# A one-core hybrid decoder step: convolution's transfers on GpSimd's queue, two kpad tiles, parameters handed out by backlog, output matrices beside input matrices

## The chip, the cores and the metric

One NeuronCore of a Trainium2 chip runs the program; the metric is its device time in microseconds (us) per execution. The kernel before took 1393.75 us, the median of 3 runs (1392.28 to 1394.62). Engines are named as in the profile: PE is TensorE (PEld its weight loads), DVE is VectorE, ACT is ScalarE, POOL is GpSimd, SP is SyncE, which here only issues transfers (SPq).

## The reference

One inference step of a hybrid layer on 256 prompt positions and 64 sampled ones (8 sequences of 8), 320 columns in all, model width 2048, all in float32:

```python
h = rmsnorm(x, g_mix)
a_val, a_gate, b_u, b_v, c_u = jnp.split(h @ w_in, [512, 1024, 1536, 2048], axis=-1)
out_a = conformer_conv(a_val, a_gate, ...)    # GLU, causal depthwise conv of 31 taps, layernorm per head, silu
out_b = chunk_spatial_gate(b_u, b_v, ...)     # u * (lower-triangular W_s v + b) in chunks of 128
out_c = s5_branch(c_u, ...)                   # complex diagonal state space, 64 groups of 16 channels, 64 states each, GLU
x = x + concat(out_a, out_b, out_c) @ w_out
gate, up = jnp.split(rmsnorm(x, g_ffn) @ w_gu, 2, axis=-1)
x = x + (silu(gate) * up) @ w_down
y = rmsnorm(x, g_final)
```

It also returns the last 30 positions of the convolution's input, the states of the state-space branch and the normalized v of the sampled part.

## The kernel before, in words

**Units.** The projections are written as a list of units. A unit loads 512 KB of weights (8 blocks of 128x128 in float32), splits them into a high part on ScalarE (`split_hi`, line 203) and a low part on VectorE (`split_lo`, line 210), and multiplies three times: high by high, high by low, low by high (lines 237, 238, 240). Loads are issued by SP three units ahead (line 1291), the high split is made two units ahead, the low one unit ahead. A tile of 128 outputs takes two units. The planner counts a block of a unit as 0.44 us of TensorE (line 247).

**Order.** First come the projections of heads 0 and 1 of the convolution, interleaved, then the string `ORDER` (line 26): `C0..C7` are the tiles of the state-space branch, `A2`, `A3` the convolution heads 2 and 3 (four units each), `K0..K3` the convolutions as matrix products, `U0..U3` the gates of the spatial mixer, `V` its eight units for v. Then the output projection (from the state-space rows first, then from the rest), then gate and up, then down.

**The planner.** All else (norm, parameters, recurrence, layout changes) is written as Python generators, handed to a planner (`Side`, line 101). Four times per unit `side.run()` lets each task of priority below 1 that is due take one step, and tasks of priority 1 or more only while the planned time of VectorE, `V.t`, isn't ahead of that of TensorE, `side.pe`. `yield Wait(n)` puts a task off by n such steps. `Vec` (line 38) adds to `V.t` a cost for each instruction. All engines get their instructions in the order in which the planner wrote them; each runs its own in order, and so does each queue.

**Convolution.** When the value projection of head h is done, VectorE writes the tile `row`; `conv_in` (line 533) copies it to DRAM (`zr<-row`) and to the output (`out_rows<-row`), reloads `row` for head h+2, and reads it back as four copies `z<-zr` of 296 KB, one per 32 channels, each with 4 shifted views (access pattern `[[1, 4], [ZW, 32], [1, Z4]]`, line 547). All are issued by SP. There is one z4 tile, so the copies for head h wait for convolution h-1 to be written.

**State-space branch.** `params()` (line 452) hands out some 110 small instructions on VectorE, three per step: exponentials, sines, the powers of the decay, and last the factor k. With k, `bb_task` (line 642) makes the input matrices' base. `c_inputs` (line 714) makes input matrices for eight channel tiles, `c_states` (line 726) multiplies the inputs by them, `recurrence` (line 770) runs the scan on VectorE in two halves. `c_mats` (line 819) makes the output matrices: its task `pool` starts after the last input matrix (flag `P`), clears three tiles on GpSimd (line 833), and per tile makes products with the powers (`powers`, line 661), which ScalarE places. TensorE multiplies (line 867), and `mat_t` (line 873) writes the result into the tile `kpad` (ScalarE line 877, VectorE line 879), copies it to DRAM (`dk<-kpad`, line 887), and reads it back shifted (line 891). There is one `kpad` tile of 224 columns, 96 of them zeros. `c_out` (line 896) applies the matrices, `c_glu` (line 930) the gates, whose weights `c_glu_w` loads.

**Norm.** `norm_task` (line 476) squares x on ScalarE, adds the squares in tiles of 1280 columns on VectorE, and gives the factor that the gates and values of the first heads wait for.

Of the kernel before, what the change touches and what calls it, by code (L numbers as in the profile page):

```python
# [24 lines left out]

ORDER = "C0 C1 C2 K0 C3 C4 C5 C6 K1 C7 A2 U0 U1 K2 A3 V K3 U2 U3".split()

# [10 lines left out]
class Vec:  # L38
# [5 lines left out]
    def _add(self, out, fixed, per):  # L44
        n = 1
        for d in out.shape[1:]:
            n *= d
        self.t += fixed + per * n

# [105 lines left out]
def _build(ctx, nc, tc, I, O):  # L155
# [142 lines left out]
    G.memset(bbd, 0.0)  # L298
    kpad = tmp("kpad", (128, 7 * 32))
    G.memset(kpad[:, 0:96], 0.0)  # L300
    cent = kp.tile([128, 128], F32, name="cent")
# [96 lines left out]
    u1, u2 = pt(), pt()  # L398

    def cmul(o, x, y):  # L400
        E.tensor_tensor(u1, pw[:, 0, x, :], pw[:, 0, y, :], op=MULT)
        E.tensor_tensor(u2, pw[:, 1, x, :], pw[:, 1, y, :], op=MULT)
        E.tensor_tensor(pw[:, 0, o, :], u1, u2, op=SUB)
        E.tensor_tensor(u1, pw[:, 0, x, :], pw[:, 1, y, :], op=MULT)
        E.tensor_tensor(u2, pw[:, 1, x, :], pw[:, 0, y, :], op=MULT)
        E.tensor_tensor(pw[:, 1, o, :], u1, u2, op=ADD)

    cmul(2, 1, 1)
    cmul(3, 2, 1)
    cmul(4, 2, 2)  # L410

    apw = tmp("apw", (128, 3, 32, 8))
    apu = tmp("t1", (128, 256)).rearrange("p (i a b) -> p i a b", i=2, a=32)
    for i in range(2):
        E.tensor_copy(apw[:, 2 - i, :, 0], pw[:, i, 4, :])
    for n in (1, 2, 4):
        x = [apw[:, 2 - i, :, 0:n] for i in range(2)]
        y = [apw[:, 2 - i, :, n - 1:n].to_broadcast([128, 32, n]) for i in range(2)]
        v1, v2 = apu[:, 0, :, 0:n], apu[:, 1, :, 0:n]
        for i, j, op in ((0, 0, SUB), (1, 1, ADD)):  # L420
            E.tensor_tensor(v1, x[0], y[j], op=MULT)
            E.tensor_tensor(v2, x[1], y[1 - j], op=MULT)
            E.tensor_tensor(apw[:, 2 - i, :, n:2 * n], v1, v2, op=op)
    E.tensor_scalar(apw[:, 0], apw[:, 1], -1.0, None, op0=MULT)
    pr, kk = pt(), tmp("kk", (128, 2, 32))
    rd = tmp("rd", (128, 32))

# [11 lines left out]
    def k_params():  # L439
# [10 lines left out]
        E.tensor_tensor(kk[:, 1, :], u1, rd, op=MULT)  # L450

    def params():
        for i, f in enumerate(E.ops[8:]):
            f()
            if i % 3 == 2:
                yield Wait(1)
        S["kk"] = True

    rd_params(E)
    k_params()  # L460

# [66 lines left out]
    def row_load(h):  # L528

        S["row", h] = tmp("row", (128, ZW), bufs=2)  # L530
        nc.sync.dma_start(S["row", h], I["rows"][h])

    def conv_in(h):

        row = zrows[h]
        yield Wait(2)
        nc.sync.dma_start(row, S["row", h])
        nc.sync.dma_start(O["rows"][h], S["row", h])
        yield Wait(5)
        if h < 2:  # L540
            row_load(h + 2)
        while h and ("k", h - 1) not in S:
            yield Wait(1)
        z4 = S["z4", h] = tmp("z4", (128, 4, Z4))
        base = row[0:1, 0:1]
        for g in range(4):
            nc.sync.dma_start(z4[:, g], bass.AP(tensor=base.tensor, offset=base.offset + 32 * g * ZW,
                                                ap=[[1, 4], [ZW, 32], [1, Z4]]))

# [81 lines left out]
    def u_layout(ct, us, du):  # L631
        U = S["U"]
        yield Wait(2)
        nc.sync.dma_start(du[:, ct % 2], us)
        if ct % 2 == 1:
            yield Wait(5)
            for j in range(4):
                nc.sync.dma_start(U[32 * j:32 * j + 32, ct - 1:ct + 1],
                                  du[:, :, j, :].rearrange("(p g) t q -> g t p q", p=4))
            S["U due", ct // 2] = side.now + 4  # L640

    def bb_task():
        while "kk" not in S:
            yield Wait(1)
        bb = S["bb"] = tmp("bb", (128, 2, 32, 16))
        w12 = tmp("wv", (128, 2, 32, 16))
        w1, w2 = w12[:, 0], w12[:, 1]
        kr, ki = bc(kk[:, 0, :]), bc(kk[:, 1, :])
        for o, x, y, op in ((0, 0, 1, SUB), (1, 1, 0, ADD)):
            V.tensor_tensor(w1, kr, bld[:, x], op=MULT)  # L650
            yield None
            V.tensor_tensor(w2, ki, bld[:, y], op=MULT)
            yield "gap"
            V.tensor_tensor(bb[:, o], w1, w2, op=op)
            yield None
        h0 = S["h0"] = tmp("wv", (128, 1536))[:, 0:512].rearrange("p (a b c) -> p a b c", a=2, b=32)
        nc.gpsimd.dma_start(h0, I["h0"])
        side.add(0.6, c_states())
        side.add(0.7, c_mats())

    def powers(E, bd, ct, src, p0, step, tags):
# [13 lines left out]
        for o, x, y, op in ((0, 0, 1, SUB), (1, 1, 0, ADD)):  # L675
            t_ = tags[2 * o:2 * o + 2] if len(tags) == 4 else tags
            v1, v2 = (tmp(t, (128, 320 if t[0] == "g" else 256))[:, 0:64 * n].rearrange("p (a b c) -> p a b c", a=4, b=n) for t in t_)
            E.tensor_tensor(v1, pb(0), xb(x), op=MULT)
            yield None
            E.tensor_tensor(v2, pb(1), xb(y), op=MULT)  # L680
# [26 lines left out]
    def c_glu_w(ct):  # L707
        for k in (ct, ct + 1):
            if k < 8 and ("wg", k) not in S:
                S["wg", k] = tmp("wg", (128, 2, 128), bufs=2)  # L710
                nc.sync.dma_start(S["wg", k], I["wglu"][k])
        return S["wg", ct]

    def c_inputs():

        src = S["src"] = [S["bb"][:, :, 4 * ct:4 * ct + 4, :] for ct in range(8)]
        for ct in range(8):
            while ct - S["T"] >= 2:
                yield Wait(1)
            for y in powers(V, bds[ct % 2], ct, src[ct], 3, -1, ("t1", "t2", "g1", "g2")):  # L720
                if y == "place":
                    yield Wait(2)
            S["b due", ct] = side.now + 3
        S["P"] = True

    def c_states():
# [6 lines left out]
        for i in range(9):  # L733
            while i < 8 and side.now < S.get(("b due", i), 1e9):
                yield Wait(1)
            if i < 8:
                power0(bds[i % 2], S["src"][i], 3)
                yield Wait(2)
            ct = i - 1
            if ct >= 0:  # L740
# [78 lines left out]
    def c_mats():  # L819
# [8 lines left out]
        def pool():  # L828
            while "P" not in S:
                yield Wait(1)  # L830
            c_raw(0)
            for t in m[:3]:
                G.memset(t, 0.0)
                yield Wait(1)
            for ct in range(8):
                while S["pow0"] < ct:
                    yield Wait(1)
                raw[ct] = r = c_raw(ct)
                while ct >= 3 and "E" not in S or ct >= 5 and S["y"] < ct - 4:
# [8 lines left out]
                V.tensor_scalar(r[:, 1], r[:, 1], -1.0, None, op0=MULT)  # L848
                for y in powers(V, bd[ct], ct, r, 1, 1, ("t1", "t2", "g1", "g2") if ct < 5 else ("t1", "t2")):
                    if y == "place":  # L850
                        yield Wait(3)
                S["pow due", ct] = side.now + 1

        side.add(0.69, pool())
        for ct in range(8):
# [3 lines left out]
            while side.now < S.get(("pow due", ct), 1e9):  # L859
                yield Wait(1)  # L860
            power0(bd[ct], raw[ct], 0)
            S["pow0"] = ct + 1
            yield Wait(3)
            pr_ = sc()
# [8 lines left out]
    def mat_t(ct, pr_, bd, two):  # L873

        while ct and ("kpad", ct - 1) not in S:
            yield Wait(1)
        A.activation(kpad[:, 128:224], pr_[:, 32:128], AF.Copy)
        yield Wait(3)
        V.scalar_tensor_tensor(kpad[:, 96:128], id32, dsk[:, ct:ct + 1], pr_[:, 0:32], op0=MULT, op1=ADD)
        if ct in (0, 1, 5, 6):  # L880
            o = 512 * (ct % 5)
            Tt = two[:, o:o + 512].rearrange("p (a b) -> p a b", a=4)
        else:
            Tt = tmp("Tt", (128, 4, 128)) if ct in (2, 7) else tmp("P", (128, 4, 128), bufs=2)
        dk = dp.tile([128, 224], F32, tag="dk", name="dk")
        yield Wait(5)
        nc.sync.dma_start(dk, kpad)
        S["kpad", ct] = True
        yield Wait(1)
        for j in range(4):  # L890
            nc.sync.dma_start(Tt[32 * j:32 * j + 32],
                              dk[:, (3 - j) * 32:(3 - j) * 32 + 128].rearrange("(p g) x -> g p x", p=4))
        S["mats"][ct] = bd, Tt
# [78 lines left out]
    def b_load():  # L972
        t = tmp("z4", (128, 2, 4, 192))
        bs, wst = S["bs"], S["wst"] = t[:, 0], t[:, 1]
        nc.sync.dma_start(bs, I["bs"].partition_broadcast(128))
        nc.sync.dma_start(wst, I["wst"])
        side.add(0.8, b_mask())
# [110 lines left out]
    def need_x():  # L1088
        if "xa" not in X:
            X["xa"] = [a4(F32, "xa") for _ in range(4)]  # L1090
            X["row"] = [X["xa"][k // 4][:, k % 4, :] for k in range(KC)]
            for q in range(4):
                nc.gpsimd.dma_start(X["xa"][q], I["xT"][:, 4 * q:4 * q + 4, :])
            side.add(6, split_ab())
# [195 lines left out]
    for u, d in enumerate(units):  # L1290
# [25 lines left out]
        if u == 4:  # L1316
            A.activation(hbgl, bgl, AF.Copy, scale=0.5)
            A.activation(nhg, cv[:, :, 1:2], AF.Copy, scale=-0.5)
            A.activation(hb, cv[:, :, 2:3], AF.Copy, scale=0.5)
        if u == 2:  # L1320
            side.add(0.9, norm_task())
        if u == 2:
            nc.sync.dma_start(bld, I["s5b"])
            row_load(0)
            row_load(1)
        if u == 0:
            side.add(0.5, params())
        if u == 9:
            side.add(0.65, bb_task())
# [118 lines left out]
```

## Time and profile before

| | |
|---|---|
| median of 3 runs | 1393.75 us (1392.28 to 1394.62) |
| the profiled execution's own time | 1393.87 us |
| its span, first to last instruction | 1392.2 us |
| PE busy | 1328.8 us (95%), 9324 matmuls |
| DVE busy | 724.3 us (52%) |
| ACT busy | 564.0 us (41%) |
| POOL busy | 58.5 us (4%) |
| mean granted clock of PE | 0.976 of full speed |
| DMA | 212.76 MB, mean 153 GB/s |

A busy PE is not PE at its peak, as its matmuls are pipelined. The granted clock of a stretch is a share of 2.4 GHz; it has two levels, 1.0 and 0.5 (1.2 GHz), and a value between is a mean over a stretch with both. A wait is named by the engine, the tile it was about to write, the line, and what it waited for. The DMA share is the mean over 16 engines.

### The profile page before, as it was taken

To read this page: it belongs to the slowest core of one execution; us is meant where nothing else is said; L and a number is where in the kernel's file an instruction comes from. 1 tells how busy PE (TensorE), PEld (TensorE's weight loads), DVE (VectorE), ACT (ScalarE), POOL (GpSimd) and SP (SyncE) were. 2 spreads that over 40 slices of the span, in tenths; PEclk is the share of its full clock that TensorE was granted. 3 is DMA by queue.
4 is the path that set the end of the run, shared out by engine and by line. 5 is a ranking of instruction groups with operands and counts; after the bars stand their busy time and mean duration, and the time that the engine had idled before them with its cause. 6 is when DMAs were issued, how large, how long until landed. Compare 5 with 4: busy or idle time off the path is not lost.

```text
span 1392.2 us, 22691 instructions
## 1 busy us (share of the span) xinstructions
PE 1328.8 (95%) x9324; PEld 1297.0 (93%) x9324; DVE 724.3 (52%) x1201; ACT 564.0 (41%) x822; POOL 58.5 (4%) x75
## 2 busy tenths in 40 slices
PE   7869879699999999999999999999999999999995
PEld 7869868489999999999999999999999999999995
DVE  7946948547556444444444444444444444444444
ACT  6356535457345433333333333333333333333442
POOL 1010000002013000000000000000000000000112
PEclk9889989899999999999999999999999999999998
DMA  6455435556444444444444444455544444554553
GB/s 232 154 173 161 128 112 166 156 148 225 152 152 151 147 141 157 146 152 152 151 152 148 152 147 152 144 153 151 151 141 163 137 161 142 153 151 144 148 147 122
DMA packets 77912, 212.76 MB, mean 153 GB/s; under 512 B 17088, under 2 KB 25536, under 8 KB 77808
## 3 DMA queue, kind: packets, MB, share of 16 engines
q1 hardware_dynamic: 76016, 205.24, 46.5%
q0 software_dynamic: 1216, 4.41, 0.9%
q8 instruction: 73, 1.20, 0.4%
q10 hardware_dynamic: 576, 1.66, 0.3%
q14 instruction: 31, 0.25, 0.1%
HBM read 202.25 MB, written 9.03 MB: 152 GB/s over the span
## 4 chain that ended last, share of the span: by engine, by line
PE 83%; DVE 8%; DMA 5%; ACT 2%; SPq 1%; issue 1%; DVEq 0%; ACTq 0%
PE acc L237 26%; PE acc L240 26%; PE acc L238 26%; DMA dk<-kpad 2%; DVE lo L52 2%; DVE lnv L52 1%; DMA raw<-in_win 1%; PE acc L568 1%; DVE H L52 1%; DVE t L52 1%; PE sc L747 1%; PE sc L907 1%; PE sc L908 1%; PE sc L909 1%; PE acc L1013 0%
## 5 line engine op out<-in xcount | busy, mean ns | idle before, releaser
L52 DVE TENSOR_TENSOR lo<-raw,hi 128x1024 fp32r<-128x1024 f32 (+1 forms) x357 | 421.4, 1182 | 224.3 <-issue 163.8
L208 ACT ACTIVATE hi<-raw 128x1024 fp32r<-128x1024 f32 (+1 forms) x361 | 369.5, 1025 | 342.7 <-PE acc L238 249.6
L237 PE MATMUL acc<-hh,hi 128*128 128x320 f32 x1408 | 424.2, 309 | 0.0
L238 PE MATMUL acc<-hl,hi 128*128 128x320 f32 x1408 | 422.8, 308 | 0.0
L240 PE MATMUL acc<-hh,lo 128*128 128x320 f32 x1408 | 321.1, 308 | 0.0
L238 PEld LDWEIGHTS acc<-hl,hi 128*128 128x128 f32 x1408 | 264.4, 188 | 0.1
L237 PEld LDWEIGHTS acc<-hh,hi 128*128 128x128 f32 x1408 | 264.2, 188 | 0.1
L240 PEld LDWEIGHTS acc<-hh,lo 128*128 128x128 f32 x1408 | 234.8, 188 | 0.0
L237 PE MATMUL acc<-fh,hi 128*128 128x320 f32 x704 | 212.0, 309 | 0.0
L238 PE MATMUL acc<-fl,hi 128*128 128x320 f32 x704 | 211.8, 308 | 0.0
L240 PE MATMUL acc<-fh,lo 128*128 128x320 f32 x704 | 165.5, 308 | 0.0
L238 PEld LDWEIGHTS acc<-fl,hi 128*128 128x128 f32 x704 | 132.1, 188 | 0.0
L237 PEld LDWEIGHTS acc<-fh,hi 128*128 128x128 f32 x704 | 132.1, 188 | 0.0
L240 PEld LDWEIGHTS acc<-fh,lo 128*128 128x128 f32 x704 | 118.9, 188 | 0.0
L52 DVE TENSOR_TENSOR xa<-acc,xa 128x320 f32<-128x320 f32 x80 | 39.3, 491 | 128.2 <-PE acc L240 128.2
L237 PE MATMUL acc<-xh,hi 128*128 128x320 f32 x288 | 92.7, 329 | 9.7 <-ACT hi L208 9.7
L238 PE MATMUL acc<-xl,hi 128*128 128x320 f32 x288 | 88.8, 316 | 0.0
L1203 ACT ACTIVATE fh<-fu 128x320 fp32r<-128x320 f32 x44 | 20.8, 472 | 163.7 <-DVE fu L52 163.7
L1181 ACT ACTIVATE fg<-fg 128x320 f32<-128x320 f32 x44 | 20.8, 472 | 138.6 <-DVE fg L52 138.6
L52 DVE TENSOR_TENSOR fu<-acc,rs 128x320 f32<-128x320 f32 x44 | 21.6, 492 | 97.9 <-PE acc L240 97.9
L52 DVE TENSOR_TENSOR fg<-acc,rs 128x320 f32<-128x320 f32 x44 | 21.6, 492 | 96.3 <-PE acc L240 96.3
L240 PE MATMUL acc<-xh,lo 128*128 128x320 f32 x288 | 67.4, 316 | 4.5 <-DVE lo L52 4.5
(255 smaller groups left out, 1356.6 us busy)
## 6 DMA issues: line engine op xcount, KB each, us to landing
raw<-in_wgu SPq DMA_DIRECT2D x176, 512.0 KB, 3.5
raw<-in_wdn SPq DMA_DIRECT2D x80, 512.0 KB, 3.6
raw<-in_win SPq DMA_DIRECT2D x37, 512.0 KB, 3.6
raw<-in_wout SPq DMA_DIRECT2D x32, 512.0 KB, 3.5
z<-zr SPq DMA_DIRECT2D x16, 296.0 KB
raw<-in_wv SPq DMA_DIRECT2D x8, 512.0 KB, 7.8
raw<-in_wdn SPq DMA_DIRECT2D x16, 256.0 KB, 2.6
xa<-in_xT POOLq DMA_DIRECT2D x4, 640.0 KB, 7.6
```

What stands on the lines that cost most here:

```text
L52: return self.v.tensor_tensor(out, a, b, op=op)
L208: A.activation(d["hi"][:, o], d["raw"][:, o], AF.Copy)
L237: T.matmul(ps, hi[:, c], r[u + j][0], start=u + j == 0, stop=False)
L238: T.matmul(ps, hi[:, c], r[u + j][1], start=False, stop=False)
L240: T.matmul(ps, lo[:, j * 128:j * 128 + 128], r[u + j][0], start=False, stop=u + j == n - 1)
L568: T.matmul(ps[c, o:o + n], w[:, 32 * (8 * g + j):32 * (8 * g + j) + 32], x, start=j == 0, stop=j == 7, tile_position=(0, 32 * g))
L747: T.matmul(pe[:, 80 * p:80 * p + 80], ps[ri][:, p, :], U[:, ct, p, :], start=True, stop=True)
L907: T.matmul(o, cat(bd[:, 0, p, 1:5]), H[:, 0, 4 * i + p, 0:80], start=True, stop=False)
L908: T.matmul(o, cat(bd[:, 1, p, 1:5]), H[:, 1, 4 * i + p, 0:80], start=False, stop=False)
L909: T.matmul(o, Tt[:, p, :], U[:, i, p, :], start=False, stop=True)
L1181: A.activation(gs, gs, AF.Silu)
L1203: A.activation(h, ub, AF.Copy)
```

## The change

It does nine things:

- `ORDER` puts K0 after C3 instead of C2, K1 after C7 instead of C6, and A3 and U1 before K2.
- All transfers of the convolution (row loads, `zr<-row`, `z<-zr`), the gates' weights `wg` and the loads of `bs` and `wst` go out on GpSimd's queue; the reload of x (`xa`) goes from GpSimd's to SP's.
- `out_rows` is written later, from DRAM to DRAM, at units 100 to 106 (in the gate and up block).
- `kpad` has two tiles of 128 columns; the DRAM copies `dk` are two fixed tiles whose 96 zero columns are written once at the start from ScalarE's queue.
- `params()` stops while `V.t` is more than 1.5 us ahead of `side.pe`; k comes before the powers, the powers 3 and 4 are made in one step, and every VectorE instruction is planned at 0.19 us at least.
- `norm_task` starts at unit 3 instead of 2; `craw` for tiles 0 and 1 is loaded at unit 6.
- The task for the output matrices no longer waits for the input matrices; it uses the scratch tiles t1, t2, the input matrices g1, g2 (before, both used four), and places the power 0 itself.
- The three tiles are cleared by ScalarE instead of GpSimd; bb's scratch is H, and `h0` is loaded later.
- Some `Wait`s are shorter, one is longer.

The diff, cut to its core:

```diff
-ORDER = "C0 C1 C2 K0 C3 C4 C5 C6 K1 C7 A2 U0 U1 K2 A3 V K3 U2 U3".split()
+ORDER = "C0 C1 C2 C3 K0 C4 C5 C6 C7 K1 A2 U0 A3 U1 K2 V K3 U2 U3".split()
-        self.t += fixed + per * n
+        self.t += max(fixed + per * n, 0.19)
-    kpad = tmp("kpad", (128, 7 * 32))
-    G.memset(kpad[:, 0:96], 0.0)
+    dks = [dp.tile([128, 224], F32, tag="dk", name="dk") for _ in range(2)]
+    for t in dks:
+        nc.scalar.dma_start(t[:, 0:96], zero[:, 0:96])
...
     def params():
         for i, f in enumerate(E.ops[8:]):
             f()
+            if i + 8 == kk_done:
+                S["kk"] = True
             if i % 3 == 2:
                 yield Wait(1)
-        S["kk"] = True
+                while V.t > side.pe + 1.5:
+                    yield Wait(1)
+        S["params"] = True
...
-        nc.sync.dma_start(S["row", h], I["rows"][h])
+        G.dma_start(S["row", h], I["rows"][h])
...
-        nc.sync.dma_start(row, S["row", h])
-        nc.sync.dma_start(O["rows"][h], S["row", h])
+        G.dma_start(row, S["row", h])
...
-            nc.sync.dma_start(z4[:, g], bass.AP(...
+            G.dma_start(z4[:, g], bass.AP(...
...
-        w12 = tmp("wv", (128, 2, 32, 16))
+        w12 = tmp("H", (128, 2, 32, 16))
...
-        h0 = S["h0"] = tmp("wv", (128, 1536))[:, 0:512].rearrange("p (a b c) -> p a b c", a=2, b=32)
-        nc.gpsimd.dma_start(h0, I["h0"])
+        while "params" not in S:
+            yield Wait(1)
...
             E.tensor_tensor(v1, pb(0), xb(x), op=MULT)
-            yield None
             E.tensor_tensor(v2, pb(1), xb(y), op=MULT)
...
-                nc.sync.dma_start(S["wg", k], I["wglu"][k])
+                G.dma_start(S["wg", k], I["wglu"][k])
...
-            for y in powers(V, bds[ct % 2], ct, src[ct], 3, -1, ("t1", "t2", "g1", "g2")):
+            for y in powers(V, bds[ct % 2], ct, src[ct], 3, -1, ("g1", "g2")):
...
         def pool():
-            while "P" not in S:
-                yield Wait(1)
-            c_raw(0)
             for t in m[:3]:
-                G.memset(t, 0.0)
-                yield Wait(1)
+                A.activation(t, ones128[:, None, 0:1].to_broadcast([128, 4, NT]), AF.Copy, scale=0.0)
+                yield None
             for ct in range(8):
-                while S["pow0"] < ct:
-                    yield Wait(1)
-                raw[ct] = r = c_raw(ct)
+                r = c_raw(ct)
                 while ct >= 3 and "E" not in S or ct >= 5 and S["y"] < ct - 4:
                     yield Wait(1)
...
-                for y in powers(V, bd[ct], ct, r, 1, 1, ("t1", "t2", "g1", "g2") if ct < 5 else ("t1", "t2")):
+                yield None
+                power0(bd[ct], r, 0)
+                for y in powers(V, bd[ct], ct, r, 1, 1, ("t1", "t2")):
                     if y == "place":
-                        yield Wait(3)
+                        yield Wait(2)
+                    else:
+                        yield None
...
-        while ct and ("kpad", ct - 1) not in S:
+        while ct > 1 and ("kpad", ct - 2) not in S:
             yield Wait(1)
-        A.activation(kpad[:, 128:224], pr_[:, 32:128], AF.Copy)
-        yield Wait(3)
-        V.scalar_tensor_tensor(kpad[:, 96:128], id32, dsk[:, ct:ct + 1], pr_[:, 0:32], op0=MULT, op1=ADD)
+        kpad = tmp("kpad", (128, 128), bufs=2)
+        A.activation(kpad[:, 32:128], pr_[:, 32:128], AF.Copy)
+        V.scalar_tensor_tensor(kpad[:, 0:32], id32, dsk[:, ct:ct + 1], pr_[:, 0:32], op0=MULT, op1=ADD)
...
-        dk = dp.tile([128, 224], F32, tag="dk", name="dk")
-        yield Wait(5)
-        nc.sync.dma_start(dk, kpad)
+        dk = dks[ct % 2]
+        yield Wait(2)
+        nc.sync.dma_start(dk[:, 96:224], kpad)
         S["kpad", ct] = True
-        yield Wait(1)
+        yield Wait(3)
...
-                nc.gpsimd.dma_start(X["xa"][q], I["xT"][:, 4 * q:4 * q + 4, :])
+                nc.sync.dma_start(X["xa"][q], I["xT"][:, 4 * q:4 * q + 4, :])
...
-        if u == 2:
+        if u == 3:
             side.add(0.9, norm_task())
+        if u in (100, 102, 104, 106):
+            h = (u - 100) // 2
+            nc.sync.dma_start(O["rows"][h], zrows[h])
...
+        if u == 6:
+            c_raw(0)
```

## Rows read from the trace of the kernel before

**Rows 1.** Windows by stretch: start:end, length, busy per engine (count), clock, DMA, GB/s.

```profile
24.00:62.00 38.00, 27.87 (x147) 26.62 (x148) 32.82 (x105) 18.35 (x28) 0.00 (x0) 0.82 0.40 130
...
62.00:86.00 24.00, 14.34 (x88) 13.85 (x87) 12.28 (x26) 5.46 (x11) 5.48 (x7) 0.79 0.58 175
...
86.00:130.00 44.00, 42.65 (x409) 40.20 (x409) 22.42 (x50) 31.22 (x62) 0.00 (x0) 1.00 0.51 161
...
130.00:172.00 42.00, 37.61 (x374) 34.63 (x373) 40.63 (x114) 21.50 (x46) 0.70 (x1) 0.99 0.44 131
...
194.00:216.00 22.00, 13.16 (x85) 8.09 (x88) 9.87 (x27) 7.02 (x14) 1.89 (x2) 0.61 0.45 142
...
246.00:254.00 8.00, 5.49 (x16) 4.22 (x17) 5.92 (x15) 5.52 (x15) 0.00 (x0) 0.79 0.59 181
...
263.50:277.00 13.50, 4.23 (x23) 2.81 (x24) 6.57 (x15) 5.95 (x16) 0.00 (x0) 0.62 0.35 112
...
345.00:1376.00 1031.00, 1031.00 (x7034) 1030.84 (x7033) 480.92 (x581) 380.01 (x466) 30.52 (x30) 1.00 0.47 148
```

**Rows 2.** Waits of PE, whole span: total us, times, longest.

```profile
PE acc L237 <- ACT hi L208: 9.7, 1, 9.7
...
PE acc L1013 <- DVE lo L52: 9.3, 1, 9.3
...
PE acc L568 <- DMA z<-zr: 7.6, 4, 3.1
...
PE sc L240 <- DVE lo L52: 5.5, 2, 4.3
...
PE acc L240 <- DVE lo L52: 4.5, 3, 3.4
...
PE sc L759 <- DVE kpad L56: 3.2, 1, 3.2
...
PE acc L1014 <- DVE gs L56: 2.7, 1, 2.7
```

**Rows 3.** Chain that ended last, in order of time: start us, us, what.

```profile
66.52 14.83 DMA raw<-in_win
...
193.74 11.76 DMA dk<-kpad
...
239.82 2.16 DMA dk<-kpad
...
255.76 13.51 DMA dk<-kpad
```

**Rows 4.** Timeline of SP's queue: start us, us, operation, count.

```profile
251.33 4.33 SPq L547 DMA_DIRECT2D z<-zr  x4
```

**Rows 5.** Windows, columns as rows 1, while only z<-zr runs.

```profile
264.00:268.00 4.00, 0.00 (x0) 0.00 (x0) 0.00 (x0) 0.00 (x0) 0.00 (x0) 0.84 0.26 101
```

**Rows 6.** Waits of all engines, whole span: total us, times, longest.

```profile
ACT kpad L877 <- DMA dk<-kpad: 28.7, 3, 14.8
...
DVE t L52 <- ACT m L688: 13.9, 3, 11.6
```

**Rows 7.** Groups of DVE, 0 to 350 us, by form: busy us, mean ns | idle before.

```profile
L52 DVE TENSOR_TENSOR t<-pw,craw 128x256 f32<-128x256 f32 x22 | 8.3, 419 | 13.9 <-ACT m L688 13.9
...
L52 DVE TENSOR_TENSOR t<-t,t 128x256 f32<-128x256 f32 x11 | 4.7, 425 | 0.4
```

**Rows 8.** Groups of ACT, 0 to 350 us, by form.

```profile
L481 ACT ACTIVATE U<-x 128x1280 f32<-128x1280 f32 x2 | 2.4, 1258 | 0.0
```

**Rows 9.** DMA issues: operation, queue, count, KB each, median us to landing.

```profile
zr<-row SPq DMA_DIRECT2D x4, 298.0 KB, 2.3
...
craw<-in_s5c POOLq DMA_DIRECT2D x8, 64.0 KB, 4.4
...
m<-dk SPq DMA_DIRECT2D x16, 64.0 KB, 1.9
...
xa<-in_xT POOLq DMA_DIRECT2D x4, 640.0 KB, 7.6
```

More of the change, by code (lines that the diff above doesn't have):

```diff
@@ L398, in _build @@
     u1, u2 = pt(), pt()
[L400 to L424, printed above, removed]
     pr, kk = pt(), tmp("kk", (128, 2, 32))
-    rd = tmp("rd", (128, 32))
+    rd = tmp("oc")[:, 0:32]
     def rd_params(V):
@@ L450, in k_params, with cmul @@
         E.tensor_tensor(kk[:, 1, :], u1, rd, op=MULT)
+    rd_params(E)
+    k_params()
+    kk_done = len(E.ops)
+    def cmul(o, x, y):
+        n = o.stop - o.start
+        v1, v2 = (v[:, 0:n] for v in (w1, w2))
+        xr, xi = (pw[:, i, x:x + 1, :].to_broadcast([128, n, 32]) for i in range(2))
+        E.tensor_tensor(v1, xr, pw[:, 0, y, :], op=MULT)
+        E.tensor_tensor(v2, xi, pw[:, 1, y, :], op=MULT)
+        E.tensor_tensor(pw[:, 0, o, :], v1, v2, op=SUB)
+        E.tensor_tensor(v1, xr, pw[:, 1, y, :], op=MULT)
+        E.tensor_tensor(v2, xi, pw[:, 0, y, :], op=MULT)
+        E.tensor_tensor(pw[:, 1, o, :], v1, v2, op=ADD)
+    w1, w2 = pt((128, 2, 32)), pt((128, 2, 32))
+    cmul(slice(2, 3), 1, slice(1, 2))
+    cmul(slice(3, 5), 2, slice(1, 3))
+    apw = tmp("apw", (128, 3, 32, 8))
+    apu = tmp("t1", (128, 256)).rearrange("p (i a b) -> p i a b", i=2, a=32)
+    for i in range(2):
+        E.tensor_copy(apw[:, 2 - i, :, 0], pw[:, i, 4, :])
+    for n in (1, 2, 4):
+        x = [apw[:, 2 - i, :, 0:n] for i in range(2)]
+        y = [apw[:, 2 - i, :, n - 1:n].to_broadcast([128, 32, n]) for i in range(2)]
+        v1, v2 = apu[:, 0, :, 0:n], apu[:, 1, :, 0:n]
+        for i, j, op in ((0, 0, SUB), (1, 1, ADD)):
+            E.tensor_tensor(v1, x[0], y[j], op=MULT)
+            E.tensor_tensor(v2, x[1], y[1 - j], op=MULT)
+            E.tensor_tensor(apw[:, 2 - i, :, n:2 * n], v1, v2, op=op)
+    E.tensor_scalar(apw[:, 0], apw[:, 1], -1.0, None, op0=MULT)
     def params():
@@ L454, in params @@
             f()
+            if i + 8 == kk_done:
+                S["kk"] = True
             if i % 3 == 2:
                 yield Wait(1)
-        S["kk"] = True
-    rd_params(E)
-    k_params()
+                while V.t > side.pe + 1.5:
+                    yield Wait(1)
+        S["params"] = True
     def bc(x, n=16):
@@ L546, in conv_in @@
         for g in range(4):
-            nc.sync.dma_start(z4[:, g], bass.AP(tensor=base.tensor, offset=base.offset + 32 * g * ZW,
-                                                ap=[[1, 4], [ZW, 32], [1, Z4]]))
+            G.dma_start(z4[:, g], bass.AP(tensor=base.tensor, offset=base.offset + 32 * g * ZW,
+                                           ap=[[1, 4], [ZW, 32], [1, Z4]]))
     def k_pre(h):
@@ L638, in u_layout @@
                 nc.sync.dma_start(U[32 * j:32 * j + 32, ct - 1:ct + 1],
-                                  du[:, :, j, :].rearrange("(p g) t q -> g t p q", p=4))
+                            du[:, :, j, :].rearrange("(p g) t q -> g t p q", p=4))
             S["U due", ct // 2] = side.now + 4
@@ L738, in c_states @@
                 yield Wait(2)
+            if i == 1:
+                h0 = S["h0"] = tmp("wv", (128, 1536))[:, 0:512].rearrange("p (a b c) -> p a b c", a=2, b=32)
+                nc.gpsimd.dma_start(h0, I["h0"])
             ct = i - 1
@@ L860, in c_mats @@
                 yield Wait(1)
-            power0(bd[ct], raw[ct], 0)
-            S["pow0"] = ct + 1
-            yield Wait(3)
             pr_ = sc()
@@ L873, in mat_t @@
     def mat_t(ct, pr_, bd, two):
-        while ct and ("kpad", ct - 1) not in S:
+        while ct > 1 and ("kpad", ct - 2) not in S:
             yield Wait(1)
-        A.activation(kpad[:, 128:224], pr_[:, 32:128], AF.Copy)
-        yield Wait(3)
-        V.scalar_tensor_tensor(kpad[:, 96:128], id32, dsk[:, ct:ct + 1], pr_[:, 0:32], op0=MULT, op1=ADD)
+        kpad = tmp("kpad", (128, 128), bufs=2)
+        A.activation(kpad[:, 32:128], pr_[:, 32:128], AF.Copy)
+        V.scalar_tensor_tensor(kpad[:, 0:32], id32, dsk[:, ct:ct + 1], pr_[:, 0:32], op0=MULT, op1=ADD)
         if ct in (0, 1, 5, 6):
@@ L884, in mat_t @@
             Tt = tmp("Tt", (128, 4, 128)) if ct in (2, 7) else tmp("P", (128, 4, 128), bufs=2)
-        dk = dp.tile([128, 224], F32, tag="dk", name="dk")
-        yield Wait(5)
-        nc.sync.dma_start(dk, kpad)
+        dk = dks[ct % 2]
+        yield Wait(2)
+        nc.sync.dma_start(dk[:, 96:224], kpad)
         S["kpad", ct] = True
-        yield Wait(1)
+        yield Wait(3)
         for j in range(4):
             nc.sync.dma_start(Tt[32 * j:32 * j + 32],
-                              dk[:, (3 - j) * 32:(3 - j) * 32 + 128].rearrange("(p g) x -> g p x", p=4))
+                        dk[:, (3 - j) * 32:(3 - j) * 32 + 128].rearrange("(p g) x -> g p x", p=4))
         S["mats"][ct] = bd, Tt
@@ L974, in b_load @@
         bs, wst = S["bs"], S["wst"] = t[:, 0], t[:, 1]
-        nc.sync.dma_start(bs, I["bs"].partition_broadcast(128))
-        nc.sync.dma_start(wst, I["wst"])
+        G.dma_start(bs, I["bs"].partition_broadcast(128))
+        G.dma_start(wst, I["wst"])
         side.add(0.8, b_mask())
```

## The prediction, made before the changed kernel ran

> **What bounds the kernel now.** I read the busy time by stretch first [rows 1], because a share over the whole span hides that the kernel has two lives. From 345 to 1376 us TensorE is busy 1031.00 us of 1031.00 at full clock; the change only adds four copies there, so this part stays. What can be won lies before 345 us, in the token mixers. For each stretch I count as lost the idle time of TensorE plus (1 - granted clock) times its busy time, which takes the clock as spread evenly over a stretch:
> - 24 to 62 us: 38.00 - 27.87 = 10.1 idle, 0.18 x 27.87 = 5.0 by the clock, 15.1 lost.
> - 62 to 86: 9.7 + 0.21 x 14.34 = 12.7.
> - 130 to 172: 4.4 + 0.4 = 4.8.
> - 194 to 216: 8.8 + 0.39 x 13.16 = 14.0.
> - 246 to 254: 2.5 + 1.2 = 3.7.
> - 263.5 to 277: 9.3 + 0.38 x 4.23 = 10.9.
>
> Together 61.2 us, the ceiling of any gain. Between them, 86 to 130 loses 1.4 us, with VectorE busy only 22.42 of 44 us.
>
> The waits of TensorE say who was late [rows 2]: a weight split on ScalarE (9.7 us, once), a split on VectorE (9.3, once), the convolution's input z (7.6 in four), splits on VectorE in the first stretch (5.5 and 4.5), the write into kpad (3.2), the tile gs (2.7). The engine named is not the cause. The chain shows what stood behind it [rows 3]: in 62 to 86 a load of weights that took 14.83 us to land; in 194 to 216 and 263.5 to 277 a copy dk<-kpad of 11.76 and 13.51 us, where the same copy took 2.16 us at 239.82. All three were issued by SP behind four copies z<-zr; those at 251.33, ahead of the copy of 255.76, are shown [rows 4]. While only those run, the DMA engines are busy by 0.26 at 101 GB/s [rows 5]: about 4 of 16 work. The four copies hold 4 x 296 KB = 1.18 MB, so 11.7 us at that rate, the size of the three late landings. A transfer behind them on SP's queue has a share for these engines and ends with them. From the DMA the wait spreads: ScalarE waits 28.7 us in three to write kpad, since the one kpad tile is still being read, and VectorE waits 13.9 us for ScalarE [rows 6], the weight splits queued behind.
>
> The Trainium skill ("DMA: Bandwidth & Descriptors", section "Why a DMA increments its semaphore by 16 and not by 1") says that a copy uses as many engines, up to 16, as divide the slowest dimension of both sides, on SP's queue the lowest-numbered, on GpSimd's consecutive ones from a moving cursor. The slowest dimension of z's source is 4, and the 0.26 agrees. By the rule z's copies, moved, would work on 16 engines and land in an estimated 3 us instead of 11.7; no run yet shows the GpSimd half. The sum below does not use it.
>
> **The change part by part.**
>
> *Convolution's copies on GpSimd's queue* (row loads, zr<-row, z<-zr, the gates' weights, the bs and wst loads). Weights and dk copies then stand behind z in no queue, though they still share four engines with it. I take the weight landing from 14.83 to the usual few us: 10 of the 12.7 in 62 to 86, and, with the next edit, 10 of the 10.9 in 263.5 to 277. The rest stays for the restart. Bounds: nothing, if sharing four engines is as slow as queueing, and 12.7 + 10.9. On GpSimd's queue, what is moved stands behind loads of craw, which wait for the readers of the tile before, and h0; else that engine has only fills and masks to do.
>
> *Two kpad tiles, and dk in two fixed DRAM tiles with the zeros written once at the start.* ScalarE waits for the copy two matrices back instead of the last one; dk<-kpad carries 64 KB instead of 112. The two zero copies go out on ScalarE's queue before x has landed, so they cost nothing; without that cover, twice the issue of a DMA.
>
> *Order.* The projection of head 3 and a gate unit now stand between head 2 and its convolution K2: eight units instead of four, 28 instead of 14 us by the planner's 0.44 x 8 per unit (line 247). z needs the steps of the waits (7 x 0.88 = 6.2 us), zr<-row (2.3, [rows 9]) and 11.7, so 20 us: late by 6 before (measured: 7.6), early by 8 after. With the kpad copy freed in the same stretch I take 12 of the 14.0. The gs wait at 246 to 254 came from head 3's gate standing right before V, whose first packing reuses that buffer; two units and a convolution lie between them after: 3 of 3.7.
>
> *Parameters by backlog, norm one unit later.* VectorE is busy 32.82 of the 38 us of the first stretch, and splits come behind the norm's sums and the parameters' small instructions. Now parameters stop while the plan has VectorE 1.5 us ahead, and each small one is planned at 0.19 us. The splits go first; the parameters take the same time but later, with k before the powers, so bb does not wait. The burst that follows the norm (gates and values of two heads) remains. Of 15.1 I take 8. Bounds: 0, if the burst decides alone, and 10.0, the waits of 5.5 and 4.5 [rows 2].
>
> *Output matrices beside input matrices.* Per matrix four products of 419 ns and two sums of 425 [rows 7]: 2.5 us. Three of the eight move from after the input matrices to beside them: 7.6 us into the stretch where VectorE has 44 - 22.4 = 21.6 us free, and out of 130 to 172, where it is busy 40.63 of 42. The write into kpad, late by 3.2 there, comes in time: 3 of 4.8. The zeroing of three tiles goes from GpSimd to ScalarE: three fills of 1280 columns, like the squares of that width 1.26 us each [rows 8], 3.8 us under ScalarE's 29% free time in 86 to 130; without that cover it delays a split once.
>
> *What it costs.* (1) VectorE has the same work in less time. At 97% busy (130 to 172) TensorE lost 4.8 - 3.2 = 1.6 us in 42; over some 130 us of such load, 5. (2) Copies on GpSimd's queue beside weights: 2; bounds 0 and the 4.4 that a craw load takes against 1.9 for 64 KB on SP [rows 9], once per head, 10. (3) x is loaded again on SP instead of GpSimd, 2.6 MB ahead of weights: it landed in 7.6 us [rows 9], weights are issued three units (10.5 us) ahead, so 1, at most 4. (4) The copies of the convolution's rows to the output move under the feed-forward block, which TensorE fills: 0. (5) A new wait at any step, as z needs h0 or parameters later than planned: 2, bounds 0 and 5.
>
> *Sum.* Gains 10 + 10 + 12 + 3 + 8 + 3 = 46, costs 5 + 2 + 1 + 2 = 10: 36 us off the profiled execution's 1393.87 us, so 1358. The median of the runs shown, 1393.75, is the same within 0.01%. A measurement of this kernel can tell about 0.2% (2.8 us) from no change.
>
> **The rivals.**
>
> *Everything lost comes back.* For: the three largest waits have one cause. Against: the burst after the norm remains. 61.2 less 4: about 1337. Chance 0.10.
>
> *VectorE becomes the bound.* For: 97% in 130 to 172, and the matrices now share two scratch tiles each where they had four, so VectorE waits for ScalarE's copies more often. Then the first stretch and 130 to 172 give nothing and cost (1) is 10: 46 - 11 - 15 = 20, so 1374. Chance 0.14.
>
> *The queue is not the cause, the four engines are.* Weights and dk wait for the same engines whoever issues z. Then 62 to 86 and 263.5 to 277 stay and 194 to 216 gives half: 46 - 10 - 10 - 6 - 8 (cost (2) is then in those waits) = 12, so 1382. Against: packets of two queues can alternate, those of one can't. Chance 0.08. The Trainium skill ("DMA: Bandwidth & Descriptors", section "Rules for kernel authors") does say that spreading copies over issuing engines brings no bandwidth; 0.26 busy shows that bandwidth isn't what lacks here.
>
> *The time is given back at the output projection.* It waits for the last gates of the state-space branch; if that chain and not TensorE sets the pace, TensorE waits there for what it saved: about 1391. Against: the chain itself stood still while ScalarE waited for kpad. Chance 0.05.
>
> *Slower: z comes late by GpSimd's queue.* Its 64 KB loads took 4.4 us against 1.9 [rows 9]. Were z's 14 us stretched by the same 2.3, it would land 32 + 6 = 38 us after its head, 10 behind each of four convolutions: 40 idle and 1.5 of slow clock each, 46; the 12 of 194 to 216 is not won: 46 - 12 - 10 - 46 = -22, so 1416. It decides from about 4.5 us late per convolution (24 / 4 - 1.5). For: z follows zr<-row and a row load, each with a wait, on one queue. Chance 0.07. The Trainium skill ("SBUF — State Buffer", section "SBUF: two separate sides") warns that VectorE can keep GpSimd from writing its descriptors; the 4.4 against 1.9 leaves room for it.
>
> **How the numbers follow.** The forecast has 0.56. Faster: 0.56 + 0.10 + 0.14 + 0.08 = 0.88. The chain's rival is 0.04 within 0.2% and 0.01 slower; with 0.07, slower 0.08. The likeliest case alone spans 1346 to 1370 (the bounds of the first stretch and of (2)). The range 1336 to 1387 takes in all the faster cases and leaves out the last two, 0.12, and some of the edges.
>
> **What would show it.** Right: no landing of weights or dk above 6 us before 345 us; ScalarE's wait to write kpad under 5 us; TensorE's wait for z gone; clock 1.00 in nearly all stretches from 60 us; the all-busy part starting near 309 us instead of 345. Wrong: TensorE waiting for z at each convolution (GpSimd), for splits with VectorE above 95% (bound), or before the output projection (chain).

## The result and the profile after

The changed kernel takes 1351.15 us, the median of 4 runs (1346.91 to 1352.68), against 1393.91 us of the kernel before in the same comparison: a ratio of 0.969, 95% interval 0.9666 to 0.9714, 42.8 us less. The forecast was 36 us less (1358, range 1336 to 1387). The profiled execution took 1352.68 us, its span is 1351.0.

The windows of the changed kernel by stretch, columns as in [rows 1]; the work in a stretch is not the same as before, since TensorE gets there sooner:

```profile
0.00:24.00 24.00, 20.98 (x115) 19.99 (x116) 17.61 (x63) 15.07 (x31) 6.62 (x17) 0.93 0.91 322
24.00:62.00 38.00, 35.22 (x236) 34.27 (x236) 35.15 (x89) 21.49 (x30) 4.99 (x8) 1.00 0.57 163
62.00:86.00 24.00, 22.29 (x233) 19.68 (x231) 14.77 (x45) 12.63 (x18) 2.96 (x5) 0.93 0.82 230
86.00:130.00 44.00, 39.73 (x312) 37.20 (x312) 31.27 (x81) 39.03 (x89) 3.89 (x6) 0.96 0.63 163
130.00:172.00 42.00, 42.00 (x415) 39.66 (x413) 38.61 (x107) 24.59 (x52) 5.94 (x8) 1.00 0.50 131
172.00:194.00 22.00, 19.60 (x144) 18.35 (x144) 18.07 (x47) 7.70 (x10) 0.59 (x1) 1.00 0.80 207
194.00:216.00 22.00, 19.49 (x219) 15.50 (x218) 16.85 (x51) 9.39 (x22) 4.08 (x6) 0.97 0.65 153
216.00:246.00 30.00, 30.00 (x159) 23.74 (x159) 21.62 (x54) 18.56 (x48) 1.63 (x3) 0.85 0.51 154
246.00:277.00 31.00, 30.31 (x305) 26.50 (x304) 19.10 (x39) 16.28 (x28) 4.97 (x12) 1.00 0.59 174
...
309.00:345.00 36.00, 36.00 (x248) 36.00 (x247) 18.57 (x25) 12.78 (x14) 0.00 (x0) 1.00 0.44 147
345.00:1334.00 989.00, 989.00 (x6748) 988.84 (x6747) 457.34 (x548) 362.20 (x444) 30.54 (x30) 1.00 0.47 150
```

By the prediction's count (idle time plus what the clock takes), 24 to 62 us loses 2.8 us where it lost 15.1, 62 to 86 loses 1.7 + 0.07 x 22.29 = 3.3 where it lost 12.7, 194 to 216 loses 3.1 where it lost 14.0, and 246 to 277 loses 0.7 where its two parts lost 3.7 and 10.9. New or larger losses are 5.9 in 86 to 130 (1.4 before), where VectorE and ScalarE now work 31.27 and 39.03 of 44 us, 2.4 in 172 to 194 (1.3 before), and 4.5 in 216 to 246, all of it by the clock, after a wait that ends at 213. From 309 to 1334 us, 17 us before the end, TensorE is never idle.

The waits of TensorE, to be held against [rows 2]:

```profile
PE acc L240 <- DVE lo L52: 4.4, 5, 1.6
PE sc L770 <- ACT H L759: 2.9, 2, 1.5
PE acc L237 <- ACT hi L208: 2.0, 2, 1.2
PE sc L949 <- issue: 1.9, 1, 1.9
PE sc L238 <- DVE xl L56: 1.7, 2, 1.3
```

None is longer than 1.9 us; the waits of 9.7 and 9.3 us, the one for z and the one for kpad are gone. But the transfers did not become quick. The chain that ended last, in order of time (compare [rows 3]), still has two loads of weights that take 12 us:

```profile
81.78 12.68 DMA raw<-in_win
...
169.21 12.09 DMA raw<-in_win
```

and the DMA issues show z itself, from GpSimd's queue, at 12.6 us, while the small dk copy is quick in the middle:

```profile
z<-zr POOLq DMA_DIRECT2D x16, 296.0 KB, 12.6
...
dk<-kpad SPq DMA_DIRECT2D x8, 64.0 KB, 1.5
```

The slowest of the eight dk copies took 8.1 us, by the instructions of the tile kpad:

```profile
DMA to landing us min/median/max: 1.5/1.5/8.1
```

Of the signs named beforehand, the wait for z is gone, ScalarE no longer waits for a dk copy (28.7 us before, [rows 6]) and the all-busy part starts at 309 us. Two signs failed: the landings stay above 6 us, and the clock is below 1.00 in four of the stretches from 62 us on. So the time is won, but not quite in the way that the prediction said. Two theories were set against each other: **queue** (weights and dk copies were late because they stood behind z) and **cover** (they are late still, and the order, the second kpad tile and the loads issued ahead hide it).

### The profile page after: what moved, and what is told of

Same layout as the page of the kernel before. It is cut to its first block, busy times and chain, and to the rows that moved or that the text cites. A ratio compares the mean times of both kernels' runs of the same rounds, so it can differ in the third digit from the quotient of the medians.

```text
span 1351.0 us, 22667 instructions
## 1 busy us (share of the span) xinstructions
PE 1318.4 (98%) x9324; PEld 1290.4 (96%) x9324; DVE 721.8 (53%) x1195; ACT 565.8 (42%) x824; POOL 71.9 (5%) x101
## 4 chain that ended last, share of the span: by engine, by line
PE 90%; DVE 4%; DMA 3%; ACT 2%; issue 1%; SPq 0%; DVEq 0%; ACTq 0%
PE acc L240 28%; PE acc L237 28%; PE acc L238 28%; DMA raw<-in_win 2%; DVE lo L52 1%; PE acc L577 1%; PE sc L758 1%; PE sc L914 1%; PE acc L1018 1%; PE sc L915 1%; PE sc L916 1%; PE acc L1020 1%; PE acc L1019 1%; PE sc L770 0%; ACT hi L208 0%
## 5 line engine op out<-in xcount | busy, mean ns | idle before, releaser
L208 ACT ACTIVATE hi<-raw 128x1024 fp32r<-128x1024 f32 (+2 forms) x361 | 369.3, 1024 | 340.1 <-PE acc L238 246.5
## 6 DMA issues: line engine op xcount, KB each, us to landing
z<-zr POOLq DMA_DIRECT2D x16, 296.0 KB, 12.6
```

What stands on the lines that cost most here:

```text
L208: A.activation(d["hi"][:, o], d["raw"][:, o], AF.Copy)
```

## The experiments

The kernel before took between 1392.84 and 1393.53 us beside them. Differences to the changed kernel are of medians; each run's ratio to the kernel before stands in brackets with its interval.

**Convolution's copies back on SP's queue** (the changed kernel, else as it is):

```diff
-        G.dma_start(S["row", h], I["rows"][h])
+        nc.sync.dma_start(S["row", h], I["rows"][h])
-        G.dma_start(row, S["row", h])
+        nc.sync.dma_start(row, S["row", h])
-            G.dma_start(z4[:, g], bass.AP(...
+            nc.sync.dma_start(z4[:, g], bass.AP(...
```

> The changed kernel with the convolution's row loads, zr<-row and z<-zr issued by SP again; all else as changed. Queue theory (weights and dk copies were late because they stood behind z on SP's queue): 15 to 20 us come back, 1366 to 1371, with weight landings of 12 us or more and TensorE waiting for weight splits over 5 us. Cover theory (in the changed kernel a weight load still took 12.68 us to land and a dk copy 8.1, so what helped is the order, the second kpad tile and the loads issued ahead): 5 us or less come back, at most 1356.

Measured: 1384.86 us (0.9938, 0.9923 to 0.9952), 33.7 us slower than the change, more than the 15 to 20 of the queue theory. The cover theory falls. Its chain, with two loads of weights that SP issued behind z:

```profile
59.94 13.89 DMA raw<-in_win
...
182.29 17.39 DMA raw<-in_win
```

and its waits of TensorE:

```profile
PE acc L237 <- ACT hi L208: 18.2, 2, 10.5
PE sc L949 <- DMA zc<-dz: 8.1, 1, 8.1
PE sc L770 <- issue: 7.7, 1, 7.7
```

A load beside z took some 12 us in the change, one behind z here takes up to 17.39, and other transfers that SP issues behind z come late too, here a copy of the gates' inputs (zc<-dz).

**One kpad tile:**

```diff
-        while ct > 1 and ("kpad", ct - 2) not in S:
+        while ct and ("kpad", ct - 1) not in S:
-        kpad = tmp("kpad", (128, 128), bufs=2)
+        kpad = tmp("kpad", (128, 128))
```

> The changed kernel with one kpad tile (a matrix's write waits for the copy of the last one). Queue theory: the copy now lands in 1.5 us in the middle, so at most 3 us come back, 1354. Cover theory: the slow copies (up to 8.1 us) hold ScalarE again, and VectorE and the weight splits behind it: about 10 us come back, 1361.

Measured: 1351.48 us (0.9703, 0.9687 to 0.972), no difference. With dk copies of 1.5 us in the middle, in this run too, the one tile is free in time. The second tile is worth nothing that can be measured here.

**The order of before:**

```diff
-ORDER = "C0 C1 C2 C3 K0 C4 C5 C6 C7 K1 A2 U0 A3 U1 K2 V K3 U2 U3".split()
+ORDER = "C0 C1 C2 K0 C3 C4 C5 C6 K1 C7 A2 U0 U1 K2 A3 V K3 U2 U3".split()
```

> The changed kernel with the order string of before. K2 stands 14 us of products after head 2 again, and V right behind head 3. Both theories: the wait for z at K2 returns (z takes 12.6 us to land on GpSimd's queue, so 6 us or more) and the gs wait of 2.7, with the clock 10 to 13 us, 1361 to 1364. If the second kpad tile and the queue had cured K2 already: 1354.

Measured: 1355.3 us (0.9723, 0.9707 to 0.974), 4.2 us slower; the interval just meets that of the change. That is less than the 10 to 13 us expected, and near the 1354 named for the case that the queue and the second tile had cured K2 already. The wait for z is back, a good half of what it was (4.8 against 7.6), and TensorE's wait for gs isn't:

```profile
PE acc L240 <- DVE lo L52: 5.4, 3, 2.9
PE acc L577 <- DMA z<-zr: 4.8, 5, 1.9
PE sc L949 <- DMA zc<-dz: 4.0, 1, 4.0
```

**Parameters without regard to the backlog, norm at unit 2:**

```diff
-                while V.t > side.pe + 1.5:
-                    yield Wait(1)
-        if u == 3:
+        if u == 2:
             side.add(0.9, norm_task())
```

> The changed kernel with parameters handed out without regard to VectorE's backlog and the norm started at unit 2 as before. Prediction's step: the first 62 us lose 8 to 12 us again, 1359 to 1363, TensorE waiting for splits. Rival (VectorE has the same work either way, so the time comes back later): within 2 us of 1351.

Measured: 1374.47 us (0.9867, 0.9847 to 0.9887), 23.3 us slower, twice what was expected. Its windows:

```profile
24.00:62.00 38.00, 28.11 (x160) 26.48 (x159) 33.38 (x104) 18.36 (x28) 5.06 (x8) 0.87 0.34 109
62.00:86.00 24.00, 16.79 (x97) 15.79 (x97) 14.33 (x31) 12.70 (x23) 0.25 (x1) 0.79 0.78 178
86.00:130.00 44.00, 36.60 (x378) 33.40 (x377) 20.28 (x51) 28.82 (x67) 6.62 (x10) 0.88 0.61 152
```

The first stretch loses 9.9 + 0.13 x 28.11 = 13.5 us (2.8 in the change), so 10.7 of it come back there, as expected. The rest is lost in the next two: 10.7 and 11.8 us against 3.3 and 5.9. In the last of them TensorE waits 7.3 us for U, read back for the states: that read-back, issued at 110.20 us, took 10.43 us beside copies of z that GpSimd issued at 106.03. (Later stretches lose and win about the same.)

**The norm alone at unit 2**, parameters paced as in the change:

```diff
-        if u == 3:
+        if u == 2:
             side.add(0.9, norm_task())
```

> The changed kernel with the norm started at unit 2 again, parameters paced as changed. Undoing both cost 23 us, of which some 10 in the first 62 us. If the norm's sums ahead of the splits are the main part: 1361 or more. If the pacing is: 1351 to 1355.

Measured: 1352.57 us (0.9718, 0.9682 to 0.9754), within the scatter of the change; the interval reaches up to 8 us above it. Its first stretch (24 to 62) loses 7.0 us against 2.8, but this doesn't reach the end. So of the 23.3 us the pacing holds most. The pacing alone was not undone.

**Output matrices after the input matrices:**

```diff
         def pool():
+            while "P" not in S:
+                yield Wait(1)
             for t in m[:3]:
```

> The changed kernel with the output matrices started only after the input matrices, as before. Prediction's step: 3 us of the write into kpad and some of VectorE's room come back lost, 1354 to 1357. Rival (VectorE is the bound from 130 us on, so 7.6 us more of work there are paid in full): 1359 or more.

Measured: 1357.2 us (0.9743, 0.9719 to 0.9768), 6.1 us slower, its runs from 1353.42 to 1360.65. The median stands just above the step's 3 to 6 us and below the rival's 8, but the interval (1353.7 to 1360.5 us) reaches both, so the run doesn't tell them apart. In the profiled execution, the slowest of the four, 172 to 194 us loses 10.1 us against 2.4: a dk copy issued at 165.03, beside z, took 16.22 us.

**The queue alone, in the kernel before** (the first diff of this section the other way round):

```diff
-        nc.sync.dma_start(S["row", h], I["rows"][h])
+        G.dma_start(S["row", h], I["rows"][h])
-        nc.sync.dma_start(row, S["row", h])
+        G.dma_start(row, S["row", h])
-            nc.sync.dma_start(z4[:, g], bass.AP(...
+            G.dma_start(z4[:, g], bass.AP(...
```

> The kernel before with one edit: the convolution's row loads, zr<-row and z<-zr on GpSimd's queue. Undoing this in the changed kernel cost 34 us. If it is worth the same by itself: about 1360. Prediction's terms for it (10 in 62 to 86, half of 12 in 194 to 216, 10 in 263.5 to 277, less 2): 24 us, 1369. If it only pays together with the order and the two kpad tiles: 1380 or more.

Measured: 1372.81 us (0.9853, 0.9833 to 0.9873), 20.7 us less than before: near the prediction's 24, and less than the 33.7 that undoing it costs. What it leaves are waits that are shorter or gone in the change:

```profile
PE sc L240 <- DVE lo L52: 5.9, 3, 5.3
PE acc L240 <- DVE lo L52: 5.1, 4, 3.6
...
PE sc L759 <- DVE kpad L56: 3.2, 1, 3.2
PE acc L1014 <- DVE gs L56: 2.7, 1, 2.7
```

**z cut by shift, in the kernel before.** Each of the four copies fills 32 partitions (one shift of all 128 channels) instead of 32 channels of all four shifts; still on SP's queue, the same bytes in the same rows:

```diff
-        for g in range(4):
-            nc.sync.dma_start(z4[:, g], bass.AP(tensor=base.tensor, offset=base.offset + 32 * g * ZW,
-                                                ap=[[1, 4], [ZW, 32], [1, Z4]]))
+        for j in range(4):
+            nc.sync.dma_start(z4[32 * j:32 * j + 32], bass.AP(tensor=base.tensor, offset=base.offset + j,
+                                                         ap=[[ZW, 32], [32 * ZW, 4], [1, Z4]]))
```

> The kernel before with one edit: the four z copies are cut by shift instead of by 32 channels (each fills 32 partitions with four rows of 592), so the slowest dimension is 32 instead of 4; still on SP's queue. Theory of few engines (weights and dk copies waited because z kept 4 of 16 engines for 12 us): z ends in 3 to 6 us, the two dk copies of 12 to 13 us fall under 6, and most of 62 to 86, 194 to 216 and 263.5 to 277 comes back: 1362 to 1372. Theory that the queue itself matters (SP's transfers behind z in any form): 1385 to 1393.

Measured: 1370.95 us (0.9836, 0.9815 to 0.9857), 21.9 us less than before by this edit alone, as much as the queue brings. Its DMA issues:

```profile
z<-zr SPq DMA_DIRECT2D x16, 296.0 KB, 7.2
...
dk<-kpad SPq DMA_DIRECT2D x8, 112.0 KB, 3.2
```

z lands in 7.2 us, the longest dk copy in 8.8 (13.51 before, under 6 expected), and ScalarE's wait to write kpad falls from 28.7 to 12.9 us:

```profile
ACT kpad L877 <- DMA dk<-kpad: 12.9, 3, 6.5
```

The queue was the cause only because of what stood in it.

**The same cut in the changed kernel, on GpSimd's queue:**

```diff
-            G.dma_start(z4[:, g], bass.AP(...  ap=[[1, 4], [ZW, 32], [1, Z4]]))
+            G.dma_start(z4[32 * j:32 * j + 32], bass.AP(...  ap=[[ZW, 32], [32 * ZW, 4], [1, Z4]]))
```

> The changed kernel with the z copies cut by shift, still on GpSimd's queue. In the changed kernel z took 12.6 us to land there although all DMA engines were busy (share 1.0 in some stretches), and weights beside it up to 12.8. If the cut is what makes z slow: z under 8 us, weights under 8 us, and the waits for ACT hi and the stretch 86 to 130 give 3 to 5 us, 1346 to 1348. If what is left is VectorE's and ScalarE's doing: 1350 to 1352.

Measured: 1344.27 us (0.9651, 0.9637 to 0.9666), 6.9 us less than the change, more than the 3 to 5 expected:

```profile
z<-zr POOLq DMA_DIRECT2D x16, 296.0 KB, 7.6
```

z is under 8 us, as expected; the longest load of weights is not (12.9), but 172 to 194 us now has no idle time. **And on SP's queue** (this cut, and the first diff of this section):

> The changed kernel with the z copies cut by shift and all of the convolution's copies on SP's queue. If the few engines were the whole cause: 1344 to 1348, as on GpSimd's queue. If what SP issues still ends behind rows and z (weights up to 10 us in the kernel before with the cut): 1353 to 1362.

Measured: 1346.62 us (0.9661, 0.9646 to 0.9675). Against the 1384.86 of the first experiment, which differs in the cut alone, 38 us less. With z cut this way, it hardly matters which queue issues it: 2.4 us between the two, with intervals that overlap.

```profile
z<-zr SPq DMA_DIRECT2D x16, 296.0 KB, 5.6
```

**The first two row loads on SP's queue at unit 2.** In the changed kernel GpSimd issues them at 5.3 us, beside the first weights:

```diff
-    def row_load(h):
+    def row_load(h, q=G):
-        G.dma_start(S["row", h], I["rows"][h])
+        q.dma_start(S["row", h], I["rows"][h])
-            row_load(0)
-            row_load(1)
+            row_load(0, nc.sync)
+            row_load(1, nc.sync)
```

> The changed kernel with the first two row loads on SP's queue at unit 2. On GpSimd's queue they go out at 5.3 us beside the first weights and x, and TensorE lost 3.0 us idle and 1.7 by the clock in the first 24 us, where it lost 2.0 before. If they cause it: 2 to 3 us faster than the change, 1348 to 1349. If not: 1350 to 1352.

Measured: 1349.0 us (0.9688, 0.9669 to 0.9707), an interval that covers the change's median. Its first stretch is as it was:

```profile
0.00:24.00 24.00, 21.13 (x117) 20.05 (x118) 17.71 (x63) 15.26 (x31) 5.55 (x15) 0.93 0.90 307
```

2.9 us idle at a clock of 0.93, against 3.0 and 0.93. The row loads on GpSimd's queue are not what slows the start. **With the cut as well:**

> The changed kernel with the z copies cut by shift and the first two row loads on SP's queue at unit 2: if the two gains of 7 and 2 us add, 1342; if the row loads' 2 us were chance, 1344.

Measured: 1344.0 us (0.9644, 0.9629 to 0.9659). The 2 us were chance or nearly so. This and 1344.27 are the fastest kernels of the study, 7 us under the change.

## Why the prediction was right, and where it was not

**The places** held, and so did the ceiling of 61.2 us. Over the first 345 us the count of idle time and clock falls from 67 us (the 61.2 of the six stretches and 6 in the others) to 28, 39 less, for 41.2 less between the two profiled executions. The sum of the terms, 36, came close because two errors pulled against each other (parameters too small, order and kpad too large), and that is luck. The span given for the likeliest case, 1346 to 1370, is not what its two named bounds make: 8 between 0 and 10.0 and 2 between 0 and 10, added, give 1354 to 1374, and the measured 1351.15 lies below that. The terms of the likeliest case were too narrow; the range of all cases held.

**The queue** was the largest term, and rightly so: it brings 20.7 us alone and costs 33.7 to undo, for a forecast of 10 + 10 + half of 12 less 2. The step that failed is "I take the weight landing from 14.83 to the usual few us", and with it the sign named for it, no landing above 6 us: loads still took 12.68 and 12.09 us. What the runs showed in its place: beside z a load takes some 12 us, behind it up to 17.39. The loads issued ahead cover nearly all of the first, but not the second, and behind z other copies of SP's queue come late too. TensorE's waits for ScalarE's splits fell from 9.7 to 2.0 us in the change and are 18.2 with the queue undone. The rival "the four engines are the cause" was half right: landings stay long beside z, and the cut of z alone brings 21.9 us in the kernel before. It was wrong that moving z then gives little. But GpSimd's queue also spreads z over more engines (last section), and no run has z on four engines of another queue than SP's: how much of the 20.7 us is due to leaving the queue and how much to the spreading stays open.

**Parameters by backlog** was the mis-sized term: 8 us taken, 10.0 as the bound. Undoing pacing and norm costs 23.3 us, the norm alone 1.4. The bound came from the two waits for splits in the first stretch; it left out the clock, and the losses of the next two stretches, where the later start put a read-back of U beside z. The first stretch alone recovered 12.3. The burst after the norm, held to remain, no longer stops TensorE for more than 1.6 us.

**Order and kpad** were over-sized. Of the 12 + 3 us the order holds 4.2, and the second kpad tile nothing that can be measured: with dk copies no longer behind z there is little left for it to cover. The terms for 194 to 216 and 263.5 to 277 had given it a part of what the queue does. The wait for gs did not return with the old order, so it is not shown that the order caused it.

**Output matrices** brought 6.1 us by undoing them, for a forecast of 3. That VectorE has room in 86 to 130 was right: 22.42 us of work there became 31.27. The stretch loses 4.5 us more, but that this is the 5 of cost (1) is not shown: the longest of TensorE's waits there, 2.9 us in two, ended with ScalarE's write of H, ScalarE is busy 39.03 of 44 us, and with the output matrices back late (VectorE busy 24.69 us) the stretch loses 7.2. The reload of x on SP cost at most 0.9 us: that is TensorE's idle time from its issue at 284 us to 309, and then there is none up to 1334.

The parts undone sum to 33.7 + 23.3 + 6.1 + 4.2 + 0.3 = 67.6 us, more than the 42.8 of the whole. The queue is worth more beside the other edits (33.7) than by itself (20.7), so the parts can't be added.

**VectorE did not become the bound**: busy 35.15 of 38 us in 24 to 62 and 38.61 of 42 in 130 to 172, it leaves TensorE a loss of 2.8 and 0 us there.

**The slower rival** (z late by GpSimd's queue) did not come: z did take 12.6 us to land there, but TensorE never waited for it. Nor did the output projection take the time back.

## What to carry to other kernels

When a small copy takes many times its usual time, look at what was issued before it on the same queue, and at the DMA share while only that runs: a low share under a full queue (here 0.26) can mean that a transfer sits on a few engines. Recutting that transfer's access pattern can be worth as much as moving it (here 21.9 and 20.7 us) and leaves the plan as it is. Background work that a planner hands out at a fixed rate should ask how far its engine is behind: the pacing of small instructions holds most of 23.3 us here.

## What was not expected of the hardware

Moved to GpSimd's queue, the copies of z did spread, but not over all engines. The windows of the changed kernel while they run show the DMA engines fully busy, where they were busy by 0.26 before [rows 5]:

```profile
52.00:60.00 8.00, 8.00 (x57) 8.00 (x56) 7.62 (x23) 1.64 (x2) 2.75 (x5) 1.00 1.01 230
...
170.00:180.00 10.00, 10.00 (x81) 9.61 (x80) 8.22 (x21) 3.00 (x7) 0.75 (x1) 1.00 1.09 190
```

That share is not z's alone. Of the 16 engines' time SP's queue, with weights, takes 51.4% and 43.9% in these two windows, and GpSimd's queue, with z and one load of rows or of craw, 49.1% and 64.5%. Counted by the packets in the traces, four of z were under way at a time through most of each set of four copies in the kernel before; in the change it is 7.0 to 8.8 in the mean of a set, and 11.9 to 13.4 with the new cut in the kernel before.

More than four agrees with what the Trainium skill ("DMA: Bandwidth & Descriptors", section "Why a DMA increments its semaphore by 16 and not by 1") says of GpSimd's cursor, which gives each copy the next engines in turn. And yet z took 12.6 us and not the 3 that were estimated from it: the mean is far from 16, and with weights beside z all engines busy moved 190 to 230 GB/s, where the first 24 us moved 322 at a share of 0.91.

The same bytes cut by shift landed in 5.6 to 7.6 us. In the old cut the four shifts of a copy read the same rows, and the four copies write the same partitions, but the packets are no slower for it: on GpSimd's queue a packet of z (4736 bytes) takes 347 ns in the median in the changed kernel and 345 with the new cut. All that this queue moves takes nearly the same time of the engines (packets, MB, share of 16 engines' span; first the changed kernel, then the same with the new cut):

```profile
q0 software_dynamic: 6176, 10.94, 3.2%
...
q0 software_dynamic: 3104, 10.91, 3.0%
```

So the new cut mainly puts more packets of z side by side, 7.0 to 12.7 in the mean of a set on GpSimd's queue. Why the old cut doesn't fill the engines there is not shown.
